# Where the squares for the first norm are taken: from GpSimd to ScalarE and VectorE in a one-core decoder layer

## The chip, the core and the metric

The kernel runs on one core of a Trainium2 chip. The metric is the device time of one execution in microseconds (us). The engines are named as in the profile: PE is TensorE (matmuls), PEld its weight loads, DVE is VectorE, ACT is ScalarE, POOL is GpSimd and SP is the engine that issues the loads. On-chip memory is SBUF, and matmuls add up in PSUM.

## The reference

One decoder layer over 256 tokens of width 2048 and a final norm, in float32. What matters here is how it begins:

```
def rms_norm(x, g):
    xf = x.astype(jnp.float32)
    y = xf * lax.rsqrt(jnp.mean(xf * xf, axis=-1, keepdims=True) + EPS)
    return (y * g.astype(jnp.float32)).astype(x.dtype)
...
        h = rms_norm(x, norm_mix[l])
        z = h @ w_in[l]
        z_a, z_b, z_cq, z_ckv_c, z_ckv_s, z_ckv_w, z_cg = jnp.split(z, split_at, axis=-1)
```

Three token mixers follow on the parts of `z`, then an output product, cross attention, a squared-ReLU MLP and the last norm. The norm's factor is one number for each token, so it can be multiplied in after the product with `w_in`, and that is what the kernel does.

## The kernel before

**Products.** Every product with a weight matrix takes its operands as two float32r parts, hi and lo = x - hi, and sums hi*hi + hi*lo + lo*hi. A weight block of 128 x 1024 numbers (512 KB) is loaded into a tile `raw`; ACT copies it to `wh` (line 82), DVE subtracts to get `wl` (line 83), and only then can PE use it. There are five `raw` buffers and three of `wh` and of `wl`, used in turn. So a load waits until the DVE is done with the block five before it, and ACT's copy waits until PE is done with the block three before it.

**The start.** `x` lies transposed in `xres`, 16 chunks of 128 features by 256 tokens. For each chunk ACT writes `hx` hi = x * gain (line 87) and DVE writes `hx` lo (line 88). The first product, `cmp`, has two accumulators (`cmp_84` and `cmp_85` in the queues below) and runs over four blocks of four chunks beside the loads of `x` and of its own eight weight blocks; the loads of the first two blocks are cut into pieces of one or two chunks. A block of one accumulator takes PE eight pairs of matmuls: one of 256 columns with `wl` (line 165) and one of 512 columns with `wh` (line 161). The second product is `k` (`acc_k0`).

**The norm.** The sum of squares over the features is kept in `ssq` (128 x 512: two chunks at a time). The first pair of chunks is squared into `ssq`; the seven others are squared into `sq` and added. `mean_eps` adds the two halves of `ssq` on POOL (line 112), multiplies by ones on PE (`pss`, line 114) and adds epsilon on DVE (`mx`); `rstd` takes the power on POOL (`rx`); `along_free` spreads it over partitions (`dg`, `psb`, `rxb`). Nothing before `rxb` needs it except the scaling of `cmp` and `k` after their products. Later norms use the same `add_squares` with the squares on ACT and the adds on POOL (lines 102 and 106).

**What sets the order.** The program is written in an order, but a scheduler at build time places the instructions in each engine's queue by its own estimate of when they can run. On the chip each queue is worked off strictly in order. The queues shown below are what it made.

Of the kernel before, what the change touches and what calls it, by code (L numbers as in the profile page):

```python
# [8 lines left out]
F32 = mybir.dt.float32  # L9
# [6 lines left out]
P = 128  # L16
S = 256
# [13 lines left out]
# column blocks of w_in that come out transposed, two 128-wide features a pair  # L31
CMP, UU, KV, CQ, BK, BQ = 0, 2, 4, 6, 10, 12
# the parts that a product in float32r takes: hi*hi, hi*lo, lo*hi
# [4 lines left out]
def trunk_kernel(ctx: ExitStack, tc: tile.TileContext, a, out):  # L38
    """Every product with a weight matrix takes its float32 operands as two float32r parts, hi and
    lo = x - hi (exact), and sums hi*hi + hi*lo + lo*hi in PSUM.  # L40

    Activations that feed a product lie transposed, [features, part, tokens], both parts side by side.
    A product comes out transposed (weights stationary, in two halves: hi*hi + lo*hi and hi*lo) or
    with tokens on partitions (activations stationary)."""
# [15 lines left out]
    # brings the activation table in before the first data  # L60
# [24 lines left out]
    def split_scaled(hi, lo, src, g):  # L85
        """hi + lo = src * g, with g one number a partition."""
        nc.scalar.activation(hi, src, AF.Copy, scale=g)
        nc.vector.scalar_tensor_tensor(lo, src, g, f32(hi), op0=ALU.mult, op1=ALU.subtract)

    def put_act(tiles, k0, src, gi):  # L90
        """src [P, n, S], features k0 .. k0 + n, times their gains."""
        for i in range(src.shape[1]):
            k = k0 + i
            t = tiles[k // 4]
            split_scaled(t[:, k % 4, 0, :], t[:, k % 4, 1, :], src[:, i, :], gT[:, gi, k:k + 1])

# [1 line left out]
    def add_squares(ssq, src, first, eng=None):  # L98
        """ssq [P, 2, S] += src ** 2."""
        sq = ssq if first else sp.tile([P, 2, S], F32, tag="sq", name="sq")  # L100
        if eng is None:
            nc.scalar.activation(sq, src, AF.Square)  # L102
        else:
            eng.tensor_tensor(sq, src, src, op=ALU.mult)
        if not first:
            nc.gpsimd.tensor_tensor(ssq, ssq, sq, op=ALU.add)  # L106

    def mean_eps(ssq, name):
        """mean over features of the squares, + eps: [P tokens, 2]."""
        s = cp.tile([P, 2], F32, name=name)  # L110
        ps = pmisc.tile([P, 2], F32, tag="sc", name="pss")
        nc.gpsimd.tensor_tensor(ssq[:, 0, :], ssq[:, 0, :], ssq[:, 1, :], op=ALU.add)
        for t in range(2):
            nc.tensor.matmul(ps[:, t:t + 1], ssq[:, 0, t * P:(t + 1) * P], ones[:, 0:1], start=True, stop=True)
        nc.vector.tensor_scalar(s, ps, 1.0 / D, EPS, op0=ALU.mult, op1=ALU.add)
        return s
# [6 lines left out]
    def along_free(r, name):  # L123
        """r [P tokens, 2] as [P, S], the same on every partition."""
        b = cp.tile([P, S], F32, name=name)
        ps = pmisc.tile([P, S], F32, tag="sc", name="psb")
        for t in range(2):
            dg = sp.tile([P, P], F32, tag="dg", name="dg")
            nc.vector.tensor_scalar_mul(dg, ident, r[:, t:t + 1])
            nc.tensor.matmul(ps[:, t * P:(t + 1) * P], ones, dg, start=True, stop=True)  # L130
        nc.scalar.activation(b, ps, AF.Copy)
        return b

# [8 lines left out]
    def gemm_t1(x, wsrc, name):  # L142
        """Like gemm_t for a contraction of 512, with one sum: [P, 2 features, tokens]."""
        acc = pacc.tile([P, 2, 2, S], F32, tag="acc", name=name)
        wh, wl = (w.rearrange("p (k n) -> p k n", k=4) for w in split_w(load_raw(wsrc)))
        for kk in range(4):
            for f in range(2):
                fs = slice(f * P, (f + 1) * P)
                for j, (w, l) in enumerate(((wh, 0), (wh, 1), (wl, 0))):
                    nc.tensor.matmul(acc[:, f, 0, :], w[:, kk, fs], x[:, kk, l, :],  # L150
                                     start=(kk == 0 and j == 0), stop=(kk == 3 and j == 2))
        return acc

    def products_t(acc, x, wh, wl, first, last):
        """acc [P, 2 features, hi*hi + lo*hi | hi*lo, tokens] += four 128-row chunks of the contraction."""
        for kk in range(4):
            for f in range(2):
                fs = slice(f * P, (f + 1) * P)

                def main(start, stop):  # L160
                    nc.tensor.matmul(acc[:, f].rearrange("p a s -> p (a s)"), wh[:, kk, fs],  # L161
                                     x[:, kk].rearrange("p a s -> p (a s)"), start=start, stop=stop)

                def low():
                    nc.tensor.matmul(acc[:, f, 0, :], wl[:, kk, fs], x[:, kk, 0, :], start=False, stop=False)  # L165

                if first and kk == 0:
                    main(True, False)
                    low()
                else:  # L170
                    low()
                    main(False, last and kk == 3)

    def gemm_t(lhs, wsrc, name, order=None, between=None):
        """Two 128-wide features, transposed: [P, 2 features, hi*hi + lo*hi | hi*lo, tokens]."""
# [9 lines left out]
    def join(acc, name, dst=None):  # L185
        """The two halves of gemm_t, added."""
# [6 lines left out]
    def gemm(lhs, wsrc, kb, n, name, between=None, hold=0):  # L193
        """Tokens on partitions: [P, 2, n]; blocks of kb 128-row chunks of the contraction. The last
        hold blocks stay, and the first tokens go through all of them before the others."""
# [67 lines left out]
    def consts(them):  # L263
        """Not ahead of the weights asked for so far."""
# [6 lines left out]
    ident = C["ident"]  # L271
    ssq = sp.tile([P, 2, S], F32, tag="ssq", name="ssq")
    for n in range(8):
        add_squares(ssq, xres[:, 2 * n:2 * n + 2, :], n == 0, nc.gpsimd)
# [6 lines left out]
    # nothing is scaled before the norm is there  # L281
    cw = slot("hC", "cw", F32).rearrange("p k a s -> p (k a s)")
    kraw = cw[:, :4 * S].rearrange("p (g s) -> p g s", g=4)
    for m, acc in enumerate(cmps):
        join(acc, "cmp", kraw[:, 2 * m:2 * m + 2, :])
    vs = slot("hC", "vs", F32).rearrange("p k a s -> p (k a s)")
    vcat = vs[:, :1024].rearrange("p (b t n) -> p b t n", b=2, t=2)
    zb = vs[:, 1024:].rearrange("p (t n) -> p t n", t=2)
    kcat = slot("hB", "kcat").rearrange("p (g a) b s -> p g a b s", g=2)
    acc_k0 = gemm_t(hx, a["w_t"][KV], "k0")  # L290
# [15 lines left out]
    # lo, hi and none: one product with hi and one with lo sum what is needed in two halves  # L306
# [6 lines left out]
    def compress():  # L313
        for m, which in enumerate(("k", "v")):
# [7 lines left out]
            # rows 0..29: hi*hi + hi*lo, rows 30..59: lo*hi  # L322
# [26 lines left out]
            else:  # L349
                # v_c of a group at the partitions 32 h of each of its heads  # L350
# [24 lines left out]
    # no compressed block lies before the first rows  # L375
# [8 lines left out]
    def softmax_pair(sc0, sc1, m0, m1, name):  # L384
        """Masked scores of two heads (or branches), both token tiles: exp(s - max) and its sums."""
# [15 lines left out]
    def scale_and_transpose(v0, v1, r, name):  # L401
        """p * r, transposed: [keys, 2, 384], the first 256 columns of keys 0..127, then 128 of the rest."""
# [20 lines left out]
    mix = [None] * 4  # L423
    for g in range(2):
# [5 lines left out]
        # compressed branch, four heads at once  # L430
# [135 lines left out]
    # w_out: the spatial gating's features last; the memory's loads among the products  # L566
# [76 lines left out]
    for q in range(4):  # L643
# [16 lines left out]
        for n in range(4):  # L660
# [3 lines left out]
            for t in range(2):  # L664
# [7 lines left out]
                if q == 3 and n == 2:  # L672
                    # what the last quarter adds comes to this
# [43 lines left out]
def _blocks(w, kb, n):  # L717
    """[K, N] -> [N / n, K / (128 kb), 128, kb * n]: what one partition reads is contiguous."""
    k = w.shape[0]
    return (w.reshape(k // (P * kb), kb, P, -1, n).transpose(3, 0, 2, 1, 4).reshape(-1, k // (P * kb), P, kb * n))  # L720


def _arrays(np, i):
# [15 lines left out]
    # cmp, u, selected k, window k, NSA q, dilated k, dilated q  # L739
# [43 lines left out]
```

## Time and profile before

| | |
|---|---|
| time of three runs | 1216.53 us median (1216.46 to 1218.69) |
| span of the profiled execution, first to last instruction | 1216.0 us |
| PE, DVE, ACT, POOL busy | 1187.0, 750.9, 588.3, 61.3 us |
| matmuls | 6450 |
| HBM read | 221.06 MB |

The profile gives the span of one execution; the three runs give whole times, whose median is 0.5 us longer than that span. Busy shares are averages over the whole program; the start, which is what the change touches, is a stretch of some 45 us of the 1216. Where a view prints "x2", two instructions stand in one row and the time is that of both.

### The profile page before, as it was taken

The page shows a single profiled execution, that of the slowest core. Times are in us where ns is not written, and L with a number is a line of the kernel's source. Part 1 is how long each engine was busy: PE and PEld are TensorE (multiplying, and loading weights), DVE is VectorE, ACT ScalarE, POOL GpSimd, SP SyncE. Part 2 cuts the span into 40 slices and gives each one's busy share as a digit, 9 for nine tenths or more (in the row PEclk, how much of TensorE's full clock was granted, in tenths as well). Part 3 has the DMA queues.
Part 4 walks back from the last instruction along what each step waited for, and adds up shares of the span by engine and source line. Part 5 has one row for each costly group of instructions (what it writes and reads, how often), then busy time and mean ns, then how long its engine had stood idle before and what let it go on. Part 6 is the DMA issues. An engine that isn't in the chain of part 4 may idle for free.

```text
span 1216.0 us, 16456 instructions
## 1 busy us (share of the span) xinstructions
PE 1187.0 (98%) x6450; PEld 1021.3 (84%) x6450; DVE 750.9 (62%) x904; ACT 588.3 (48%) x800; POOL 61.3 (5%) x54
## 2 busy tenths in 40 slices
PE   5999999999999999999999999999999999999996
PEld 4899888888878888988888888888888888888885
DVE  8775788467687565865554556554565555566554
ACT  5464555365565455644433444433444433444443
POOL 7000000000033100200000000000000000000000
PEclk9999999999999999999999999999999999999999
DMA  6676533555657555555666655666556566655663
GB/s 228 196 252 209 157 122 122 182 158 172 190 191 224 176 172 174 181 177 192 189 195 191 191 186 182 192 201 193 187 178 192 191 196 195 186 185 185 195 189 104
DMA packets 65385, 224.24 MB, mean 184 GB/s; under 512 B 7963, under 2 KB 9499, under 8 KB 65179
## 3 DMA queue, kind: packets, MB, share of 16 engines
q1 hardware_dynamic: 65307, 223.19, 57.8%
q8 instruction: 50, 0.82, 0.3%
q14 instruction: 28, 0.23, 0.1%
HBM read 221.06 MB, written 2.10 MB: 184 GB/s over the span
## 4 chain that ended last, share of the span: by engine, by line
PE 91%; DVE 4%; issue 2%; ACT 1%; DMA 1%; SPq 0%; ACTq 0%; POOLq 0%; POOL 0%; DVEq 0%
PE dn L207 27%; PE up L161 20%; PE up L165 10%; PE wo L161 3%; PE cq L161 2%; DVE wl L83 2%; PE xo L150 2%; PE bv L207 2%; PE v L207 2%; PE mv L207 2%; PE wo L165 2%; PE cq L165 1%; PE xq L161 1%; PE mk L161 1%; PE u L161 1%
## 5 line engine op out<-in xcount | busy, mean ns | idle before, releaser
L83 DVE TENSOR_TENSOR wl<-raw,wh 128x1024 fp32r<-128x1024 f32 (+3 forms) x414 | 505.2, 1224 | 350.5 <-ACT wh L82 348.8
L82 ACT ACTIVATE wh<-raw 128x1024 fp32r<-128x1024 f32 (+3 forms) x414 | 428.8, 1038 | 459.9 <-PE dn L207 185.5
L161 PE MATMUL up<-h,wh 128*128 128x512 f32 x1024 | 359.3, 398 | 0.0
L207 PE MATMUL dn<-wh,hid 128*128 128x512 f32 x992 | 306.2, 389 | 0.0
L165 PE MATMUL up<-h,wl 128*128 128x256 f32 x1024 | 282.4, 281 | 0.0
L161 PEld LDWEIGHTS up<-h,wh 128*128 128x128 f32 x1024 | 190.6, 188 | 44.1
L207 PEld LDWEIGHTS dn<-wh,hid 128*128 128x128 f32 x992 | 186.2, 188 | 38.4
L165 PEld LDWEIGHTS up<-h,wl 128*128 128x128 f32 x1024 | 193.3, 189 | 2.7
L207 PE MATMUL dn<-wl,hid 128*128 128x512 f32 x496 | 193.1, 389 | 0.6 <-DVE sf L675 0.6
L207 PEld LDWEIGHTS dn<-wl,hid 128*128 128x128 f32 x496 | 93.1, 188 | 20.5 <-DVE wl L83 1.0
L161 PE MATMUL wo<-mix,wh 128*128 128x512 f32 x256 | 89.5, 395 | 0.4 <-ACT wh L82 0.4
L165 PE MATMUL wo<-mix,wl 128*128 128x256 f32 x256 | 70.7, 282 | 3.3 <-DVE wl L83 3.3
L161 PEld LDWEIGHTS wo<-mix,wh 128*128 128x128 f32 x256 | 47.5, 188 | 10.9 <-ACT wh L82 0.7
L165 PEld LDWEIGHTS wo<-mix,wl 128*128 128x128 f32 x256 | 48.3, 189 | 5.2 <-DVE wl L83 4.5
L188 ACT ACTIVATE half<-up 128x512 f32<-128x512 f32 x32 | 19.1, 597 | 56.7 <-PE up L161 56.7
L161 PE MATMUL cq<-hx,wh 128*128 128x512 f32 x128 | 45.5, 397 | 0.0
L190 DVE TENSOR_TENSOR half<-up,half 128x512 f32<-128x512 f32 x32 | 22.1, 692 | 35.5 <-ACT half L188 35.5
L106 POOL TENSOR_TENSOR ssq<-ssq,sq 128x512 f32<-128x512 f32 x21 | 30.6, 1456 | 174.6 <-ACT sq L102 174.2
L680 POOL TENSOR_TENSOR rf<-sf,mhalf 128x1 f32<-128x1 f32 x2 | 1.1, 560 | 706.8 <-DVE sf L678 706.8
L165 PE MATMUL cq<-hx,wl 128*128 128x256 f32 x128 | 35.3, 281 | 0.0
L161 PE MATMUL cmp<-hx,wh 128*128 128x512 f32 x64 | 27.6, 463 | 4.6 <-ACT wh L82 4.6
L666 DVE SCALAR_TENSOR_TENSOR xt<-dn,m,xt 128x512 f32<-128x512 f32 x32 | 22.6, 747 | 14.3 <-PE dn L207 14.3
(282 smaller groups left out, 1409.9 us busy)
## 6 DMA issues: line engine op xcount, KB each, us to landing
raw<-in_w_up SPq DMA_DIRECT2D x128, 512.0 KB, 4.3
raw<-in_w_down SPq DMA_DIRECT2D x128, 512.0 KB, 4.3
raw<-in_w_t SPq DMA_DIRECT2D x52, 512.0 KB, 3.6
raw<-in_w_out SPq DMA_DIRECT2D x32, 512.0 KB, 4.3
raw<-in_w_bv SPq DMA_DIRECT2D x8, 512.0 KB, 3.7
raw<-in_w_v SPq DMA_DIRECT2D x8, 512.0 KB, 3.5
raw<-in_w_mk SPq DMA_DIRECT2D x8, 512.0 KB, 4.2
raw<-in_w_q SPq DMA_DIRECT2D x8, 512.0 KB, 3.8
```

The lines of the kernel that those rows point to most:

```text
L82: nc.scalar.activation(hi, src, AF.Copy)
L83: nc.vector.tensor_tensor(lo, src, f32(hi), op=ALU.subtract)
L106: nc.gpsimd.tensor_tensor(ssq, ssq, sq, op=ALU.add)
L150: nc.tensor.matmul(acc[:, f, 0, :], w[:, kk, fs], x[:, kk, l, :], start=(kk == 0 and j == 0), stop=(kk == 3 and j == 2))
L161: nc.tensor.matmul(acc[:, f].rearrange("p a s -> p (a s)"), wh[:, kk, fs], x[:, kk].rearrange("p a s -> p (a s)"), start=start, stop=stop)
L165: nc.tensor.matmul(acc[:, f, 0, :], wl[:, kk, fs], x[:, kk, 0, :], start=False, stop=False)
L188: nc.scalar.activation(lo, acc[:, :, 1, :], AF.Copy)
L190: nc.vector.tensor_tensor(d, acc[:, :, 0, :], lo, op=ALU.add)
L207: nc.tensor.matmul(acc[t][:, :n], lhs[k // 4][:, k % 4, l, ts], w[:, kk, :], start=(k == 0 and j == 0), stop=(k == KD - 1 and j == 2))
L666: nc.vector.scalar_tensor_tensor(xs, acc[t], r3[:, t:t + 1], xs, op0=ALU.mult, op1=ALU.add)
L680: nc.gpsimd.tensor_tensor(rf, s_, mhalf[:, 0:1], op=ALU.pow)
```

## The change

The squares of all eight pairs of chunks are taken by ACT (`Square`), and the seven adds for this norm run on DVE. They are written in a generator that the second product calls between its blocks, with the two joins of `cmp` ahead of them; the steps from `mean_eps` to `nrx` are written after the second product. Later norms keep their adds on POOL.

```
-    def add_squares(ssq, src, first, eng=None):
-        """ssq [P, 2, S] += src ** 2."""
+    def add_squares(ssq, src, first, add=None):
         sq = ssq if first else sp.tile([P, 2, S], F32, tag="sq", name="sq")
-        if eng is None:
-            nc.scalar.activation(sq, src, AF.Square)
-        else:
-            eng.tensor_tensor(sq, src, src, op=ALU.mult)
+        nc.scalar.activation(sq, src, AF.Square)
         if not first:
-            nc.gpsimd.tensor_tensor(ssq, ssq, sq, op=ALU.add)
+            (add or nc.gpsimd).tensor_tensor(ssq, ssq, sq, op=ALU.add)
...
     ssq = sp.tile([P, 2, S], F32, tag="ssq", name="ssq")
-    for n in range(8):
-        add_squares(ssq, xres[:, 2 * n:2 * n + 2, :], n == 0, nc.gpsimd)
+
+    def squares():
+        for m, acc in enumerate(cmps):
+            join(acc, "cmp", kraw[:, 2 * m:2 * m + 2, :])
+        for b in range(4):
+            for n in (2 * b, 2 * b + 1):
+                add_squares(ssq, xres[:, 2 * n:2 * n + 2, :], n == 0, add=nc.vector)
+            yield
+
+    acc_k0 = gemm_t(hx, a["w_t"][KV], "k0", between=squares())
     rx = rstd(mean_eps(ssq, "mx"), "rx")
     rxb = along_free(rx, "rxb")
...
-    for m, acc in enumerate(cmps):
-        join(acc, "cmp", kraw[:, 2 * m:2 * m + 2, :])
...
-    acc_k0 = gemm_t(hx, a["w_t"][KV], "k0")
```

Where the scheduler puts this is not where it is written. The first place is DVE's queue during the first product, from block 1 (`hx_81` is the second of the four `hx` tiles) to the weights of block 2 (128x1024). Before:

```order
L88 SCALAR_TENSOR_TENSOR hx_81<-xres,gT,hx_81 128x256 x2
L83 TENSOR_TENSOR wl<-raw,wh 128x512 x2
L88 SCALAR_TENSOR_TENSOR hx_81<-xres,gT,hx_81 128x256 x2
L83 TENSOR_TENSOR wl<-raw,wh 128x512 x2
L88 SCALAR_TENSOR_TENSOR hx_82<-xres,gT,hx_82 128x256 x4
L83 TENSOR_TENSOR wl<-raw,wh 128x1024 x2
```

After the change (the adds have line 103 there):

```order
L88 SCALAR_TENSOR_TENSOR hx_81<-xres,gT,hx_81 128x256 x2
L103 TENSOR_TENSOR ssq<-ssq,sq 128x512
L83 TENSOR_TENSOR wl<-raw,wh 128x512
L88 SCALAR_TENSOR_TENSOR hx_81<-xres,gT,hx_81 128x256
L83 TENSOR_TENSOR wl<-raw,wh 128x512
L88 SCALAR_TENSOR_TENSOR hx_81<-xres,gT,hx_81 128x256
L103 TENSOR_TENSOR ssq<-ssq,sq 128x512
L83 TENSOR_TENSOR wl<-raw,wh 128x512 x2
L88 SCALAR_TENSOR_TENSOR hx_82<-xres,gT,hx_82 128x256 x4
L103 TENSOR_TENSOR ssq<-ssq,sq 128x512 x2
L83 TENSOR_TENSOR wl<-raw,wh 128x1024 x2
```

So four adds stand ahead of the weights of block 2, inside the first product; one more stands ahead of these rows and two behind them. ACT's queue changes in the same way: its eight squares (line 101 after the change) stand behind the `hx` pieces of their own chunks, all in the first product, and no further table load appears.

The second place is PE's queue at the end of the first product. Before, the product with ones stands behind the whole of it:

```order
L161 MATMUL cmp_85<-hx_83,wh 128x512
L165 MATMUL cmp_85<-hx_83,wl 128x256
L161 MATMUL cmp_85<-hx_83,wh 128x512
L114 MATMUL pss<-ones,ssq 128x1 x2
L161 MATMUL k_383<-hx_80,wh 128x512
```

After the change it stands ahead of the last eight pairs:

```order
L158 MATMUL cmp_84<-hx_83,wh 128x512
L162 MATMUL cmp_84<-hx_83,wl 128x256
L158 MATMUL cmp_84<-hx_83,wh 128x512
L111 MATMUL pss<-ones,ssq 128x1 x2
L162 MATMUL cmp_85<-hx_83,wl 128x256
```

It moved forward past eight pairs of matmuls; the matmuls of `psb`, which stood in the second product, moved forward by twelve matmuls. POOL's queue loses its first fifteen tensor instructions. SP's queue, with every load, is the same in both, and so is all that comes behind the second product but for one copy on ACT and one subtraction on DVE that each move by a place.

## Rows read from the trace of the kernel before

**Rows 1.** The page: span, busy time of the engines, POOL's busy tenths by slice.

```profile
span 1216.0 us, 16456 instructions
...
PE 1187.0 (98%) x6450; PEld 1021.3 (84%) x6450; DVE 750.9 (62%) x904; ACT 588.3 (48%) x800; POOL 61.3 (5%) x54
...
POOL 7000000000033100200000000000000000000000
```

**Rows 2.** What PE waited for, whole span: us in total, times, longest.

```profile
PE cmp L165 <- DVE wl L83: 9.7, 4, 3.9
PE cmp L161 <- ACT wh L82: 4.6, 1, 4.6
PE wo L165 <- DVE wl L83: 3.3, 3, 1.7
```

**Rows 3.** Busy us by stretch; the last three columns: granted clock, DMA share, GB/s.

```profile
10.44:11.90 1.46, 0.73 (x4) 0.68 (x5) 1.22 (x3) 0.67 (x2) 0.00 (x0) 1.00 0.92 302
...
17.20:28.50 11.30, 6.91 (x28) 5.16 (x26) 11.30 (x9) 5.74 (x10) 11.08 (x9) 0.85 0.62 199
```

**Rows 4.** DVE by form, 6 to 31 us: count, busy us, mean ns, idle before.

```profile
L88 DVE SCALAR_TENSOR_TENSOR hx<-xres,gT,hx 128x256 fp32r<-128x256 f32 x11 | 13.2, 1244 | 1.6 <-ACT hx L87 1.6
L83 DVE TENSOR_TENSOR wl<-raw,wh 128x512 fp32r<-128x512 f32 x6 | 8.0, 1362 | 0.2 <-ACT wh L82 0.2
```

**Rows 5.** DVE by form, 31 to 62 us.

```profile
L88 DVE SCALAR_TENSOR_TENSOR hx<-xres,gT,hx 128x256 fp32r<-128x256 f32 x4 | 1.7, 472 | 0.0
...
L302 DVE TENSOR_TENSOR cw<-cw,rxb 128x512 f32<-128x512 f32 x2 | 1.3, 690 | 0.4 <-ACT rxb L131 0.4
```

**Rows 6.** DVE in order of time: start, us, instruction, idle time before it.

```profile
8.17 2.35 DVE L88 SCALAR_TENSOR_TENSOR hx<-xres,gT,hx 128x256 fp32r<-128x256 f32 x2 [0.25 <-ACT hx L87]
10.44 0.68 DVE L83 TENSOR_TENSOR wl<-raw,wh 128x512 fp32r<-128x512 f32 x1
...
12.40 2.27 DVE L88 SCALAR_TENSOR_TENSOR hx<-xres,gT,hx 128x256 fp32r<-128x256 f32 x2 [0.34 <-ACT hx L87]
...
28.64 2.88 DVE L83 TENSOR_TENSOR wl<-raw,wh 128x1024 fp32r<-128x1024 f32 x2
...
33.03 1.21 DVE L83 TENSOR_TENSOR wl<-raw,wh 128x1024 fp32r<-128x1024 f32 x1
```

**Rows 7.** ACT's squares of later norms, line 102: least, median, most ns.

```profile
L102 ACT ACTIVATE sq<-xres x14: 617/618/621, 325.3 to 498.3; 128x512 f32<-128x512 f32 x14
```

**Rows 8.** PE in order of time.

```profile
16.17 0.39 PE L165 MATMUL cmp<-hx,wl 128*128 128x256 f32 x1 [1.95 <-DVE wl L83]
...
21.89 0.39 PE L165 MATMUL cmp<-hx,wl 128*128 128x256 f32 x1 [2.37 <-DVE wl L83]
...
30.43 0.58 PE L165 MATMUL cmp<-hx,wl 128*128 128x256 f32 x1 [3.92 <-DVE wl L83]
...
36.27 0.39 PE L161 MATMUL cmp<-hx,wh 128*128 128x512 f32 x1
...
43.90 0.39 PE L161 MATMUL cmp<-hx,wh 128*128 128x512 f32 x1
44.12 0.50 PE L114 MATMUL pss<-ones,ssq 128*128 128x1 f32 x4
```

**Rows 9.** ACT in order of time.

```profile
11.86 0.91 ACT L87 ACTIVATE hx<-xres,gT 128x256 fp32r<-128x256 f32 x2 [0.53 <-DMA xres<-in_xT]
...
14.03 0.91 ACT L87 ACTIVATE hx<-xres,gT 128x256 fp32r<-128x256 f32 x2
14.85 1.17 ACT L82 ACTIVATE wh<-raw 128x512 fp32r<-128x512 f32 x2
...
18.29 1.05 ACT L82 ACTIVATE wh<-raw 128x1024 fp32r<-128x1024 f32 x1
```

**Rows 10.** POOL in order of time: the addition of the two halves of `ssq`.

```profile
28.51 0.79 POOL L112 TENSOR_TENSOR ssq<-ssq 128x256 f32<-128x256 f32 x1
```

**Rows 11.** SP's queue in order of time: the last two loads of the first product.

```profile
13.39 8.80 SPq L253 DMA_DIRECT2D raw<-in_w_t  x2
```

More of the change, by code (lines that the diff above doesn't have):

```diff
@@ L271, in trunk_kernel @@
     ident = C["ident"]
-    ssq = sp.tile([P, 2, S], F32, tag="ssq", name="ssq")
-    for n in range(8):
-        add_squares(ssq, xres[:, 2 * n:2 * n + 2, :], n == 0, nc.gpsimd)
+    cw = slot("hC", "cw", F32).rearrange("p k a s -> p (k a s)")
+    kraw = cw[:, :4 * S].rearrange("p (g s) -> p g s", g=4)
+    vs = slot("hC", "vs", F32).rearrange("p k a s -> p (k a s)")
+    vcat = vs[:, :1024].rearrange("p (b t n) -> p b t n", b=2, t=2)
+    zb = vs[:, 1024:].rearrange("p (t n) -> p t n", t=2)
+    kcat = slot("hB", "kcat").rearrange("p (g a) b s -> p g a b s", g=2)
+    ssq = sp.tile([P, 2, S], F32, tag="ssq", name="ssq")
+    def squares():
[6 more added lines that the diff above has]
+    acc_k0 = gemm_t(hx, a["w_t"][KV], "k0", between=squares())
     rx = rstd(mean_eps(ssq, "mx"), "rx")
@@ L280, in trunk_kernel @@
     nc.vector.tensor_scalar_mul(nrx, rx, -1.0)
-    cw = slot("hC", "cw", F32).rearrange("p k a s -> p (k a s)")
-    kraw = cw[:, :4 * S].rearrange("p (g s) -> p g s", g=4)
-    for m, acc in enumerate(cmps):
-        join(acc, "cmp", kraw[:, 2 * m:2 * m + 2, :])
[L286 to L289, printed above, removed]
-    acc_k0 = gemm_t(hx, a["w_t"][KV], "k0")
     consts([("cau", [P, S]), ("mcmp", [P, 2, NCMP]), ("mB", [P, 384]), ("bs", [P, NB]), ("triu", [P, P])])
```

## The prediction

> **What bounds the kernel now.** I read four views: the page, the list of PE's waits, tables by stretch and by form, and the engines in order of time through the first 45 us. The page shows PE busy for 98% of the span, and POOL busy almost only at the very start [rows 1]. The list of waits says where PE's few idle microseconds are: 9.7 us behind DVE's `wl` and 4.6 us behind ACT's first `wh` (the very first data), both in the first product; the next entry in all that follows is 3.3 us [rows 2]. So whatever the first product gives up moves the rest forward, and there is no slack behind it to swallow the gain.
>
> Inside the first product PE is not short of columns but of split weights, and those come from DVE, which is busy 11.30 of the 11.30 us from 17.20 to 28.50 [rows 3]. It is slow there: an instruction of line 88 on 128x256 takes 1244 ns on average between 6 and 31 us [rows 4] and 472 ns behind 31 us [rows 5]; the 128x512 form of line 83 averages 1362 ns [rows 4], but 0.68 us at 10.44 [rows 6]. That last row decides what to blame. It lies in a gap of POOL: from 10.44 to 11.90 POOL did nothing, the DMA engines were 92% busy, and DVE ran at its normal pace. From 17.20 to 28.50 the DMA share is lower, 0.62, POOL works 11.08 of 11.30 us, and DVE crawls [rows 3]. DVE is slow when POOL works, whatever the loads do.
>
> **The change part by part.**
>
> *Removed from POOL:* eight squares and seven adds, all its tensor work of the first product. None of it is on the path; what counts is that DVE's instructions go back to their undisturbed durations.
>
> *Added:* eight squares on ACT, 617 ns each where the same form runs later [rows 7], and seven adds of 128x512 on DVE. For these the nearest row is line 302, two in 1.3 us [rows 5]; I take 0.66. Both stand inside the first product, not beside the second as they are written, so they count against the path.
>
> A rule speaks against this half of the change. The row has DVE saturated, 11.30 of 11.30 us [rows 3]. The Trainium skill (Perfetto Trace Analysis, section Optimizing Scalar/DVE Operations) advises to take work off a saturated DVE, even to GpSimd, though it doubts that trading between these two helps because they share a read port. By its advice alone, seven adds more on DVE at the durations now seen make the kernel slower, 1220.8; by the rows with and without POOL they are paid back several times, 1206.0. Both are worked out below.
>
> *The path to block 2.* PE's last wait in the first product ends at 30.43 [rows 8], when the first `wl` of block 2 is there: DVE began it, with its twin, at 28.64 [rows 6]. I follow DVE's new queue from the last point that the loads fix. At 11.86 a piece of `x` lands and ACT makes `hx` hi [rows 9]; DVE's line 88 follows at 12.40 [rows 6]. From there to block 2's first `wl` the new queue holds eight of line 88, four 128x512 of line 83, four adds and the 128x1024 itself. Undisturbed, 8 x 0.45 + 4 x 0.64 + 4 x 0.66 + 1.21 = 10.0 us, so it ends at 22.4, and PE starts at 22.5: **7.9 us earlier**. (1.21 is the row at 33.03; 0.45 lies between 1.7 / 4 and 0.472; 0.64 between half of 1.21 and 0.68 [rows 5, 6].) With the lowest of these it is 22.0, with the highest 22.9.
>
> ACT has to keep up. The next piece of `x` was taken without a wait at 14.03, so it had landed. From there ACT's queue to block 2's first `wh` holds two of line 87, three weights of 128x512, four of line 87, three squares and 1.05 us: 0.9 + 1.75 + 1.8 + 1.85 + 1.05 = 7.4 us [rows 7, 9], so 21.4. DVE's queue reaches that `wl` at 22.4 - 1.2 = 21.2. A tie; I stay at 22.4 and allow 1 us above.
>
> *The clock.* Behind 30.43 PE runs without a wait to 44.12, 13.7 us for 32 pairs. At the full clock a pair takes (43.90 - 36.27) / 22 = 0.347 us [rows 8], so 32 take 11.1. The difference of 2.6 us is a stretch at the 1.2 GHz level after waits of 1.95, 2.37 and 3.92 us; the granted clock is already down to 0.85 on average from 17.20 to 28.50 [rows 3]. Now PE restarts block 0 at 10.5 (8.17 plus two of line 88, an add and a `wl`), has done its last eight pairs at 13.3, waits 1.3 us for block 1 at 14.6, and 2.3 us from 20.2 to 22.5 for block 2. Before, it had waited 9.7 - 3.9 = 5.8 us by 22 and fell; now it will have waited some 4.3, with 0.8 ahead of 10.5. I take full speed: **2.6 us gained**.
>
> *The product with ones* costs PE the same at its new place, but it needs the seventh add and 0.79 us on POOL [rows 10]. Behind 22.4 DVE's queue is 1.21 + 4 x 0.45 + 0.66 + 1.21 + 0.66: `wl` of block 3 is there at 27.3, the add at 27.9, POOL's sum at 28.8. PE wants the weights at 22.5 + 16 x 0.347 = 28.1 and the sum at 30.8. Cost zero, hidden behind blocks 2 and 3, with 0.8 and 2.0 us in hand; if either were later, every matmul behind it would wait as long.
>
> *The loads.* The last two weight blocks of the first product were held up on SP, 8.80 us from 13.39 [rows 11], because a `raw` buffer came free only when DVE had split its contents. Now that is done near 17.4. Even with 4 us to land the block is there at 22, wanted by ACT near 26. SP's order is unchanged.
>
> *Sum.* The first product ends at 22.5 + 11.1 = 33.6 instead of 44.12 [rows 8]: 10.5 us, 7.9 of them from DVE and 2.6 from the clock. Behind it the queues are the same but for three single places, and PE was busy there and stays so. The profiled execution's 1216.0 [rows 1] becomes 1205.5; the median of the three runs lies 0.5 above that span, so **1206.0**.
>
> **The rivals.**
>
> *PE at half clock again.* For it: it fell after a wait of 2.37 us [rows 8], and one of 2.3 is left. Against: the sum of waits is smaller. Price: up to the 2.6 us above, so 1208.6; 1207.3 for half of it.
>
> *All at the lower rows.* `wl` at 22.0 and ACT no brake, or `rxb` early enough to save a wait behind: 0.5 to 2 us more, 1204 to 1205.5. For it: four of line 88 take 1.7 us together [rows 5]. Against: ACT's tie.
>
> *DVE gets seven adds and nothing back* (the other side). If the slow stretch comes from the loads or from DVE itself, line 88 stays at 1244, line 83 at 1362, and the adds cost 1362 too: from 12.40, 8 x 1.24 + 4 x 1.36 + 4 x 1.36 + 2.88 / 2 = 22.2, so 34.6 instead of 30.3, 4.3 us later: 1220.8. It decides from the point where line 88 keeps more than about 0.9 us, since 8 x (0.87 + 1.22) + 1.21 fills the time to 30.3. For it: DVE is full. Against: the gap of POOL at 10.44 with the loads at 0.92 [rows 3].
>
> *Something behind takes it back.* The weights of `k` may be no earlier, as every load waits for a buffer and every `wh` for PE; PE would then stand at 34. For it: the buffers couple all engines. Against: they come free on DVE's times, which move forward by the same 8 to 10 us. Half the gain lost is 1211, all of it 1216.5.
>
> **How the numbers follow.** The forecast, 1205.5 to 1207, has 0.52; half clock (1207 to 1209.5) 0.19; the lower rows (1203 to 1205.5) 0.15; taken back (1209.5 to 1217) 0.10, a third of it within 2.4 us of no change; DVE burdened 0.03; 0.01 lies beyond. The range 1203.0 to 1210.0 holds the first three and a little of the fourth. 0.2% (2.4 us) is about what a measurement of this kernel can tell from no change. Faster by more than that 0.93, within it 0.04, slower 0.03.
>
> **What would show it.** In the changed kernel line 88 averages 0.42 to 0.48 us ahead of 31 us, the 128x512 subtraction 0.6 to 0.7, the added lines about 0.66 on DVE and 0.6 on ACT, and POOL does no tensor work before the sum of the halves. PE's last wait in the first product ends near 22.5, `k` starts near 34, and the granted clock stays at the 2.4 GHz level from 10 us on. I am wrong if line 88 stays above 0.9 us with POOL idle, if PE stands ahead of the moved product with ones or of block 3, if ACT and not DVE is what DVE's `wl` waits for over a us, or if a wait of some us stands behind 34 that was not there.

## The result, and the profile of the changed kernel

The changed kernel takes **1206.24 us** (median of four runs, 1205.78 to 1206.72), beside 1217.23 us for the kernel before in the same comparison: a ratio of 0.9901 by the comparison's own estimate, with a 95% interval of 0.9888 to 0.9915 (the two medians alone give 0.9910). The forecast was 1206.0, and its steps can be looked up in the new trace.

The page of the changed kernel, to set against [rows 1]: span, PE's busy time, POOL's busy tenths in 40 slices of 30 us.

```profile
span 1204.7 us, 16460 instructions
...
PE 1183.8 (98%) x6450; PEld 1018.5 (85%) x6450; DVE 743.3 (62%) x911; ACT 592.2 (49%) x808; POOL 42.9 (4%) x39
...
POOL 0000000000123001100000000000000000000000
```

POOL's first slice went from 7 to 0, and DVE, which took over seven adds, is busy for 743.3 us instead of 750.9. With more instructions it works less: its others have become shorter. DVE by form from 6 to 31 us says which, and answers to [rows 4]:

```profile
L88 DVE SCALAR_TENSOR_TENSOR hx<-xres,gT,hx 128x256 fp32r<-128x256 f32 x14 | 6.1, 480 | 1.6 <-ACT hx L87 1.6
...
L103 DVE TENSOR_TENSOR ssq<-ssq,sq 128x512 f32<-128x512 f32 x7 | 4.8, 686 | 0.2
L83 DVE TENSOR_TENSOR wl<-raw,wh 128x512 fp32r<-128x512 f32 x6 | 4.0, 686 | 0.2 <-ACT wh L82 0.2
```

Line 88 fell from 1244 to 480 ns, the 128x512 subtraction from 1362 to 686. The seven adds cost 4.8 us. What that does for PE is in the list of its waits ([rows 2] before):

```profile
PE cmp L158 <- ACT wh L82: 4.3, 1, 4.3
PE wo L162 <- DVE wl L83: 3.1, 3, 1.6
PE cmp L162 <- DVE wl L83: 2.3, 3, 1.6
```

9.7 us behind `wl` in the first product have become 2.3. In PE's order of time (against [rows 8]) these are three waits, and the last ends at 22.00 instead of 30.43:

```profile
10.46 0.39 PE L162 MATMUL cmp<-hx,wl 128*128 128x256 f32 x1 [0.33 <-DVE wl L83]
...
13.93 0.38 PE L162 MATMUL cmp<-hx,wl 128*128 128x256 f32 x1 [0.38 <-DVE wl L83]
...
22.00 0.38 PE L162 MATMUL cmp<-hx,wl 128*128 128x256 f32 x1 [1.63 <-DVE wl L83]
...
30.59 0.50 PE L111 MATMUL pss<-ones,ssq 128*128 128x1 f32 x4
...
33.85 0.40 PE L158 MATMUL k<-hx,wh 128*128 128x512 f32 x1
```

`k`, the second product, starts at 33.85 us. In the trace of before, PE in order of time:

```profile
44.49 0.47 PE L161 MATMUL k<-hx,wh 128*128 128x512 f32 x1
```

So 10.6 of the 11.3 us by which the span is shorter come from the first product, and 0.7 from behind it. The granted clock stands in the last but two column of the busy times by stretch ([rows 3] before); here the stretches 10:20, 20:30 and 30:34:

```profile
10.00:20.00 10.00, 9.22 (x49) 7.29 (x48) 8.83 (x17) 8.33 (x18) 0.00 (x0) 1.00 1.01 391
20.00:30.00 10.00, 8.37 (x49) 7.02 (x48) 8.99 (x13) 7.12 (x11) 1.66 (x1) 1.00 0.88 268
30.00:34.00 4.00, 4.00 (x26) 3.53 (x25) 2.88 (x8) 1.55 (x2) 0.71 (x1) 1.00 0.94 218
```

1.00 in all three is the 2.4 GHz level, where the trace of before shows 0.85 on average from 17.20 to 28.50 and half speed again behind its last long wait, which ended at 30.43. Busy times by stretch, before:

```profile
32.00:36.00 4.00, 4.00 (x15) 3.42 (x14) 2.24 (x4) 0.04 (x1) 0.00 (x0) 0.51 0.79 266
```

### The profile page after: what moved, and what is told of

It reads as the page before. It is cut to its first block, busy times and chain, and to the rows that moved or that the text cites. A ratio compares the mean times of both kernels' runs of the same rounds, so it can differ in the third digit from the quotient of the medians.

```text
span 1204.7 us, 16460 instructions
## 1 busy us (share of the span) xinstructions
PE 1183.8 (98%) x6450; PEld 1018.5 (85%) x6450; DVE 743.3 (62%) x911; ACT 592.2 (49%) x808; POOL 42.9 (4%) x39
## 4 chain that ended last, share of the span: by engine, by line
PE 92%; DVE 3%; DMA 2%; issue 1%; ACT 1%; SPq 0%; ACTq 0%; POOLq 0%; POOL 0%; DVEq 0%
PE dn L204 27%; PE up L158 20%; PE up L162 10%; PE wo L158 3%; PE cq L158 2%; PE xo L147 2%; PE bv L204 2%; PE v L204 2%; PE mv L204 2%; PE wo L162 2%; DVE wl L83 1%; PE cq L162 1%; PE xq L158 1%; PE u L158 1%; PE bk L158 1%
## 5 line engine op out<-in xcount | busy, mean ns | idle before, releaser
L158 PE MATMUL cmp<-hx,wh 128*128 128x512 f32 x64 | 25.1, 431 | 4.3 <-ACT wh L82 4.3
L82 ACT ACTIVATE hid<-half 128x512 fp32r<-128x512 f32 x32 | 20.2, 632 | 17.1 <-DVE half L651 17.1
L158 PEld LDWEIGHTS cq<-hx,wh 128*128 128x128 f32 x128 | 23.9, 188 | 5.1
```

The lines of the kernel that those rows point to most:

```text
L82: nc.scalar.activation(hi, src, AF.Copy)
```

## The experiments

A theory had to be told apart from its rivals. Mine: POOL's work beside DVE holds up DVE's instructions, and PE waits for DVE. The rivals: it is the work itself that counts (moved to where there is room), or its place in the program (beside the first or the second product). A finer question is whether POOL's being busy is enough, or whether it has to read SBUF. Each comparison carries its own runs of the kernel before, whose medians lay between 1216.8 and 1218.0.

**a_adds_pool: only half of the change.** The squares are on ACT, the adds stay on POOL.

```diff
-                add_squares(ssq, xres[:, 2 * n:2 * n + 2, :], n == 0, add=nc.vector)
+                add_squares(ssq, xres[:, 2 * n:2 * n + 2, :], n == 0)
```

> Squares on ACT as changed, but the seven adds stay on POOL: half of POOL's tensor work of the first product is back. Theory (POOL's work slows DVE): seven adds of about 1.4 us are 10 us of POOL work instead of 20, each holding DVE up by some 0.8 us (1244 - 472 ns); DVE itself loses the adds. From 12.4 to block 2's first wl 8 x 0.45 + 4 x 0.64 + 1.21 = 7.4 us and four or five hold-ups of 0.8, so 23.0 to 23.6 instead of 22.0: 1207 to 1209 us, line 88 at 0.6 to 0.9 us ahead of 31 us. Rival (the slow stretch came from the loads or from DVE itself): DVE has the queue of the kernel before, so 1216 to 1217.

Measured: 1208.78 us (1207.61 to 1209.32), ratio 0.9932 [0.9918, 0.9946]. With half of POOL's reading left, line 88 stands about halfway between 480 and 1244 ns (DVE by form, 6 to 31 us):

```profile
L88 DVE SCALAR_TENSOR_TENSOR hx<-xres,gT,hx 128x256 fp32r<-128x256 f32 x15 | 11.1, 789 | 2.4 <-ACT hx L87 2.4
```

PE waits 4.2 us for `cmp`'s `wl` instead of 2.3, and the clock is near its lower level twice, at 0.53. Busy times by stretch:

```profile
11.80:15.30 3.50, 3.50 (x13) 2.98 (x12) 2.18 (x3) 3.28 (x8) 1.28 (x1) 0.53 1.05 420
25.50:28.90 3.40, 3.40 (x12) 2.88 (x12) 3.40 (x5) 0.45 (x1) 2.60 (x2) 0.53 0.81 258
```

So the seven adds cost 4.8 us when they are on DVE, and having them there is still worth 2.5 us of the kernel's time (by the medians of two comparisons), which is the opposite of what a count of DVE's work says.

**c_junk_reads: POOL's reading put back, with no use.** The changed kernel, and beside it 15 multiplications of 128x512 on POOL whose result nobody reads. The other engines' work is unchanged.

```diff
+    junk = cp.tile([P, 2, S], F32, name="junk")
+    nc.gpsimd.memset(junk, 0.0)
+    for i in range(15):
+        nc.gpsimd.tensor_tensor(junk, junk, xres[:, 0:2, :], op=ALU.mult)
```

> The changed kernel with fifteen multiplications of 128x512 on POOL whose result nobody uses, from about 6 us on; the queues of DVE, ACT and PE are those of the changed kernel. Theory: line 88 is back at 1.2 us and the adds on DVE take about 1.36, block 2's first wl comes at 34 to 35, the clock falls again: 1219 to 1223 us, slower than the kernel before. Rival (the gain came from the new order of the queues and from the moved product with ones): 1206 to 1207, the product with ones at most 1 or 2 us late behind POOL's queue.

Measured: 1217.82 us (1216.08 to 1219.36), ratio 1.0005 [0.9996, 1.0015]: the whole gain is gone. DVE by form from 6 to 28.5 us, while the multiplications ran:

```profile
L88 DVE SCALAR_TENSOR_TENSOR hx<-xres,gT,hx 128x256 fp32r<-128x256 f32 x7 | 10.0, 1450 | 0.9 <-ACT hx L87 0.9
L83 DVE TENSOR_TENSOR wl<-raw,wh 128x512 fp32r<-128x512 f32 x4 | 6.9, 1753 | 0.0
L103 DVE TENSOR_TENSOR ssq<-ssq,sq 128x512 f32<-128x512 f32 x2 | 3.5, 1760 | 0.0
```

POOL's side of the same time, 6 to 31 us:

```profile
L279 POOL TENSOR_TENSOR junk<-junk,xres 128x512 f32<-128x512 f32 x15 | 21.6, 1441 | 5.1 <-DMA xres<-in_xT 4.0
```

Each of DVE's instructions took about its own time plus one of POOL's: line 88's 0.48 us and 1.04 us, which one such multiplication takes when it starts before DVE (it is in d_junk_writes below), make 1.52 for the 1.45 seen, and line 83's 0.69 and 1.04 make 1.73 for 1.75. That is what two engines that take turns would give.

The time came out 1 us under the range, although PE started block 2 at 34.81, as expected. The multiplications were over at 28.5 us, and the granted clock fell once only (0.50 from 26 to 32 us) and was at 1.00 from 33 us on, so PE ran from that start at full speed; in the kernel before it ran there at 0.51. So the new order of the queues is not what gains, and POOL's work need not be of any use to take the gain back. Whether it is POOL's reading or its being busy, this run does not tell; the next one does.

**d_junk_writes: POOL as busy, but only writing.** One operation that reads, and then 40 memsets of the same 128x512.

```diff
+    nc.gpsimd.tensor_tensor(junk, xres[:, 0:2, :], xres[:, 0:2, :], op=ALU.mult)
+    for i in range(40):
+        nc.gpsimd.memset(junk, 0.0)
```

> The same with forty memsets of 128x512 on POOL, which write SBUF and read nothing, about 0.5 us each, 16 to 20 us in all over the first product. If any work of POOL holds DVE up, line 88 is above 1 us again and the kernel takes 1214 to 1222 us. If only reading does (as the Trainium skill, SBUF - State Buffer, section on its two separate sides, has it for DVE instructions with two SBUF inputs), line 88 stays at 0.48 and the time at 1206 us, within 1 us.

Measured: 1205.3 us (1204.23 to 1208.17), ratio 0.9908 [0.9893, 0.9923], the time of the changed kernel. DVE by form and POOL by form, both from 6 to 31 us:

```profile
L88 DVE SCALAR_TENSOR_TENSOR hx<-xres,gT,hx 128x256 fp32r<-128x256 f32 x15 | 7.0, 508 | 1.4 <-ACT hx L87 1.4
...
L83 DVE TENSOR_TENSOR wl<-raw,wh 128x512 fp32r<-128x512 f32 x6 | 4.0, 689 | 0.0
```

```profile
L279 POOL MEMSET junk<- 128x512 f32 x37 | 19.5, 526 | 2.1
...
L277 POOL TENSOR_TENSOR junk<-xres 128x512 f32<-128x512 f32 x1 | 1.0, 1040 | 3.8 <-DMA xres<-in_xT 3.8
```

19.5 us of POOL's work cost DVE nothing (the mean of 508 ns holds one of 0.90 us at 5.57, beside the one operation that reads). "POOL is busy" is not the cause; that it reads SBUF is. (POOL's reading work in all these runs has two inputs; no run tried one with a single input.)

**e_behind: the squares where the text has them.** In the changed kernel they stand in the code beside the second product, but the scheduler put them inside the first. Here they are queued on ACT behind the first product's last weight copy (`last` in the cut below), and the adds run on DVE from 25.1 to 35.1 us.

```diff
+                with tc.issue_after(last):
+                    add_squares(ssq, xres[:, 2 * n:2 * n + 2, :], n == 0, add=nc.vector)
```

> The squares as they are written in the change: queued on ACT behind the last weight copy of the first product, so squares and adds stand beside the second product. Theory: DVE's queue to block 2's first wl loses four adds and ACT's three squares; wh of block 2 at about 19.5, wl at 20.8, PE starts 1.1 to 1.6 us earlier than 22.0; if DVE has room in the second product the kernel takes 1204.6 to 1205.6 us. Rival (the place that the scheduler chose is part of the gain): the norm's factor comes late, DVE is full from 34 to 50 us, PE waits there: 1207 to 1211 us.

Measured: 1210.54 us (1210.25 to 1211.31), ratio 0.9949 [0.9936, 0.9961]. My expectation failed and the rival held. The first product did get faster (`k` at 31.16), but the norm came late. ACT's copy of `rxb`, and PE in the product that follows on the second one (its tiles are named `k` too), both in order of time:

```profile
46.82 0.37 ACT L130 ACTIVATE rxb<-psb 128x256 f32<-128x256 f32 x1
```

```profile
52.92 0.58 PE L164 MATMUL k<-hx,wl 128*128 128x256 f32 x1 [3.87 <-DVE wl L85]
```

In the changed kernel, ACT in order of time:

```profile
37.80 0.37 ACT L128 ACTIVATE rxb<-psb 128x256 f32<-128x256 f32 x1
```

There PE waits for nothing in this product. In e_behind what is scaled by `rxb` stands in one piece ahead of the next `wl`, 3.6 us of DVE's work from 48.09 on. PE waits 3.87 us, and the granted clock is 0.50 from 51 to 57. DVE's piece is not the whole of that wait. ACT's copy and DVE's subtraction for the block that PE waits for, both in order of time:

```profile
49.08 1.06 ACT L84 ACTIVATE wh<-raw 128x1024 fp32r<-128x1024 f32 x1 [1.89 <-PE k L160]
```

```profile
51.66 1.21 DVE L85 TENSOR_TENSOR wl<-raw,wh 128x1024 fp32r<-128x1024 f32 x1
```

The copy ended at 50.14, so DVE's piece cost 1.5 us. The other 2.3 passed because the copy began only when PE had finished the block before. Of the three `wh` buffers the other two, by the order in which they are used, held weights of the product `ph`, which needs the norm (its operand `blk` is made from what `rxb` has scaled) and ran from 58.06 on (in the changed kernel from 48.20).

**b_all_dve: squares and adds both on DVE.** POOL and ACT have none of it.

```diff
-        nc.scalar.activation(sq, src, AF.Square)
+        if add is None:
+            nc.scalar.activation(sq, src, AF.Square)
+        else:
+            add.tensor_tensor(sq, src, src, op=ALU.mult)
```

> Squares and adds both on VectorE, GpSimd idle, ScalarE without squares. Theory (only GpSimd's reading held VectorE up): line 88 stays at 0.45 to 0.55 us and a 128x512 subtraction at 0.69; VectorE carries eight squares of about 0.69 us more, four of them ahead of block 2's first wl, so TensorE starts block 2 some 2 to 3 us later than the 22.0 of the changed kernel, near 24.5, and then half a us to a us goes at block 3: 1208.5 to 1211 us. Rival 1 (it only counts that GpSimd is left, whoever takes the work): 1206, the same as the changed kernel. Rival 2 (VectorE full with all of the work is no better than the kernel before): 1215 to 1218.

Measured: 1213.7 us (1212.4 to 1214.27), ratio 0.9966 [0.9954, 0.9978]: slower than my range, and the price lay elsewhere than I had put it. Line 88 is at 479 ns. DVE is busy for 19.86 of the 20 us from 10 to 30, yet PE starts block 2 at 22.19, as in the changed kernel, and `k` at 33.61. PE in order of time:

```profile
22.19 0.38 PE L165 MATMUL cmp<-hx,wl 128*128 128x256 f32 x1 [1.30 <-DVE wl L83]
...
33.61 0.39 PE L161 MATMUL k<-hx,wh 128*128 128x512 f32 x1
...
36.42 0.50 PE L114 MATMUL pss<-ones,ssq 128*128 128x1 f32 x4
...
45.34 0.60 PE L130 MATMUL psb<-dg,ones 128*128 128x128 f32 x4
...
54.87 0.58 PE L165 MATMUL k<-hx,wl 128*128 128x256 f32 x1 [3.33 <-DVE wl L83]
```

The last add ends at 31.9 instead of 27.0, so PE's products with ones stand behind the first block of `k`, and `rxb` comes at 46.98, 9.2 us later than in the changed kernel. About 4 of these 9 us are added by places in PE's queue: POOL's sum was there at 32.70 and `pss` ran at 36.42, `dg` was there at 39.33 and `psb` ran at 45.34 (in the changed kernel 28.74 and 30.59, 32.59 and 36.64). It is the same lateness as in e_behind, again with a wait of over 3 us, and a granted clock of 0.82 and 0.75 in the 8 us behind 52. Taking work off POOL pays even when all of it goes to DVE, but the squares on ACT are worth another 7.5 us. The first product is as fast without that, so the loss lies behind it, where the norm is late.

**f_pool_behind: all of it on POOL, but beside the second product.** A tiny operation ahead of them in POOL's queue reads the first product's sums; `add_squares` is that of b_all_dve.

```diff
+        go = nc.gpsimd.tensor_tensor(gate_, kraw[:, 0, 0:2], kraw[:, 0, 0:2], op=ALU.mult)
...
+                with tc.issue_after(go.ins):
+                    add_squares(ssq, xres[:, 2 * n:2 * n + 2, :], n == 0, add=nc.gpsimd)
```

> All fifteen squares and adds stay on GpSimd, but a tiny operation that reads the first product's sums stands ahead of them in GpSimd's queue, so that they run beside the second product, where the changed kernel's text has them. Theory (VectorE is held up wherever GpSimd reads beside it, and the norm is late): the first product is as fast as with no squares at all (block 2 starts near 21, k near 33), but from 33 to about 55 us line 83 and line 88's neighbours on VectorE take about twice their time, the 128x1024 subtraction 2.2 us or more instead of 1.2, rxb comes 15 us or more later than 37.8, and TensorE waits 5 us or more in the second product and what follows: 1212 to 1222 us. Rival (the contention matters only in the first product, where VectorE is short): 1204.5 to 1206.

Measured: 1223.04 us (1221.79 to 1224.62), ratio 1.0046 [1.0029, 1.0063]: slower than before, 1 us over my range. The first product was fast (`k` at 31.82). Then POOL reads from 30.65 to 56.5, and DVE in order of time shows whom it holds up:

```profile
32.84 0.68 DVE L190 TENSOR_TENSOR cw<-cmp,half 128x512 f32<-128x512 f32 x1
...
35.90 2.23 DVE L83 TENSOR_TENSOR wl<-raw,wh 128x1024 fp32r<-128x1024 f32 x1 [1.00 <-ACT wh L82]
...
43.76 0.69 DVE L190 TENSOR_TENSOR half<-k,half 128x512 f32<-128x512 f32 x1 [0.40 <-ACT half L188]
```

The subtraction of line 83 takes 2.23 us instead of 1.22, but line 190, which adds a PSUM tile and one SBUF tile, keeps its 0.69. And the norm is 25 us late (`rxb` at 62.36), for which PE stands still, in the list of its waits:

```profile
PE ph L339 <- DVE blk L83: 6.5, 1, 6.5
PE k L165 <- DVE wl L83: 4.6, 2, 3.4
...
PE psb L130 <- DVE dg L129: 2.3, 1, 2.3
```

So POOL's reading holds DVE up beside either product, and together with the late norm it costs more than the first product gives; this run does not part the two.

**h_own_block: each block's squares behind that block's weights.** A middle way between the changed kernel and e_behind: two squares fewer ahead of block 2's `wl` (`ends[b]` is the last weight copy of block b).

```diff
+                with tc.issue_after(ends[b]):
+                    add_squares(ssq, xres[:, 2 * n:2 * n + 2, :], n == 0, add=nc.vector)
```

> The changed kernel with the squares of each block queued on ScalarE behind the last weight copy of their own block, so that two squares and a VectorE add or two fewer stand ahead of block 2's first wl, and the norm is hardly later. Theory (VectorE's queue sets block 2's start): block 2's first wl and TensorE's start come 0.7 to 1.5 us earlier than 22.0, and as rxb is later by under 2 us nothing behind waits for it: 1204.5 to 1205.5. Rival (what is gained there is lost behind, as with the squares queued behind the first product): 1206 to 1208.

Measured: 1206.25 us (1205.87 to 1207.2), ratio 0.9909 [0.9894, 0.9924]: no gain, the rival held. Both halves are in PE's order of time:

```profile
20.76 0.38 PE L162 MATMUL cmp<-hx,wl 128*128 128x256 f32 x1 [1.06 <-DVE wl L83]
...
49.50 0.38 PE L162 MATMUL k<-hx,wl 128*128 128x256 f32 x1 [1.53 <-DVE wl L83]
```

Block 2 starts 1.24 us earlier, as expected, and 1.53 us are lost at 49.50. `rxb` is 1.4 us later (39.23), and DVE is busy for 12.00 of the 12 us from 40 to 52, as it is in the changed kernel too. So PE arrives earlier at weights that are not earlier: DVE begins that subtraction at 48.24, and the one in its place in the changed kernel at 47.92. Behind the first product DVE has no slack either.

**g_no_pool_adds, i_later_only, after_again, g_again: the same cause elsewhere.** In both kernels the adds of three later norms are on POOL, 21 in all; two of these norms lie beside the `w_out` product (325 to 370 us and further on), the third at 468 to 490 us, where PE hardly waits (0.2 us at `xo`, in g too). g moves all 21 to DVE in the changed kernel (the diff below, and g_again is the same kernel); i does it in the kernel before and leaves the first norm as it was there; after_again is the changed kernel.

```diff
-            (add or nc.gpsimd).tensor_tensor(ssq, ssq, sq, op=ALU.add)
+            (add or nc.vector).tensor_tensor(ssq, ssq, sq, op=ALU.add)
```

> The changed kernel with the adds of the later norms on VectorE too, where they are on GpSimd in both kernels (325 to 368 us and further on). Theory: the few waits of TensorE on VectorE's wl at line 162 beside these adds (3.1 us in all, with line 83's 128x1024 at 1366 ns there and line 88 at 609 to 702) come of the same contention and shrink to under 1 us, the 128x1024 subtraction goes to 1.2 us, and the time to 1203 to 1205.5. Rival (TensorE is the bound there and VectorE gets the work back that it sheds): within 0.5 us of the changed kernel, 1205.5 to 1206.7; slower than that if the 16 or more adds make VectorE late.

> The kernel before, with only the adds of the two later norms moved from GpSimd to VectorE (the first norm stays on GpSimd as it was). Theory (GpSimd's reading costs wherever TensorE waits for VectorE's wl, and the two places are independent): the first product is slow as before (k starts near 44.5), the waits of TensorE at line 165 in the w_out product (3.3 us before) go, with 0.4 at line 161, so 1212.5 to 1214 us, and the gains of the two places add up to that of the kernel that has both. Rival (the 3.6 us by which the kernel with both beat the changed one came from elsewhere, such as earlier loads): 1216 to 1218.

> The changed kernel once more, beside the next one on the same chip: 1205.5 to 1207 us.

> The changed kernel with the later norms' adds on VectorE too, beside the changed kernel on the same chip: if the waits at the w_out product are what it saves, 3 to 4 us less than the changed kernel in this same call, 1202 to 1203.5; if the difference was one of chips, under 1 us less.

Measured: g 1202.62 us (1201.22 to 1204.13), ratio 0.9882 [0.9861, 0.9902]. In a second comparison, on one chip: before 1217.95, i 1214.16 (1212.63 to 1214.73; ratio 0.9966 [0.9953, 0.9979]), the changed kernel 1205.37 (1204.75 to 1206.72; 0.9900 [0.9883, 0.9917]), g 1201.74 (1201.54 to 1203.14; 0.9869 [0.9855, 0.9883]). The two places add up: 3.8 us for i and 12.6 for the change make 16.4, and g has 16.2. Four of these times lie a little outside what I had expected, by 0.1 to 0.4 us: both of g and that of the changed kernel below it, that of i above it. DVE by form from 300 to 375 us, first of the changed kernel and then of g:

```profile
L83 DVE TENSOR_TENSOR wl<-raw,wh 128x1024 fp32r<-128x1024 f32 x26 | 35.0, 1366 | 9.6 <-ACT wh L82 9.6
...
L88 DVE SCALAR_TENSOR_TENSOR h<-xres,gT,h 128x256 fp32r<-128x256 f32 x14 | 9.3, 702 | 0.0
```

```profile
L83 DVE TENSOR_TENSOR wl<-raw,wh 128x1024 fp32r<-128x1024 f32 x28 | 34.2, 1233 | 8.7 <-ACT wh L82 8.7
...
L88 DVE SCALAR_TENSOR_TENSOR h<-xres,gT,h 128x256 fp32r<-128x256 f32 x14 | 6.1, 481 | 0.0
```

PE's busy time in that stretch, of the changed kernel and of g (the second number is the length, the third PE's):

```profile
300.00:375.00 75.00, 71.14 (x405) 61.20 (x404) 60.41 (x70) 46.84 (x71) 21.04 (x14) 1.00 0.62 204
```

```profile
300.00:375.00 75.00, 75.00 (x431) 65.42 (x431) 61.62 (x87) 48.17 (x73) 1.44 (x2) 1.00 0.64 214
```

The 3.9 us of idle PE, listed as waits for `wo`, are gone (0.4 of them are left in g_again), and i's list has none behind `wl` there either. g is the fastest version here.

## Why the prediction was right, point by point

**DVE was slow because of POOL.** Right, and shown by c, which takes the gain back with work on POOL alone, and by d, in which as much work that does not read takes nothing back. The gap of POOL in [rows 6] was the right row to read. The rival in which DVE gets the adds and nothing back would have needed line 88 above 0.9 us; it is at 0.48. A refinement that the prediction lacked: POOL has to read (d), and DVE's instruction has to take two inputs from SBUF (line 190 in f). The Trainium skill states both conditions (SBUF — State Buffer, section SBUF: two separate sides): the ports are a lock that a VectorE operation with two SBUF inputs contends for, against a GpSimd operation that reads SBUF; the rows of c, d and f agree.

**Durations.** A little low: 480 ns for 450, 686 for 640 and 660, 1.22 us for 1.21.

**Block 2's `wl` at 22.4, PE at 22.5.** Measured 22.00. The queue from line 88 on took 10.5 us instead of 10.0, of which DVE idled 0.7, but it began at 11.39 instead of 12.40, since ACT got that piece of `x` at 10.85 instead of 11.86. So the 8.4 us gained here, for 7.9, come in part of a piece that happened to land a microsecond earlier. In the runs with this same queue that row of line 88 begins anywhere from 11.01 (d_junk_writes) to 12.62 (g_again), and after_again, the same program, started block 2 at 21.16: executions differ by a microsecond here.

**ACT as a tie.** ACT's two copies for block 2 took 2.00 us from 19.41, so the first ended near 20.4, a microsecond ahead of the 21.4 worked out; ACT was no brake.

**The clock.** Right in kind, a little large: the three stretches from 10 to 34 us are all at 1.00, but from block 2's start to `k` PE took 11.85 us (22.00 to 33.85) instead of 14.06 (30.43 to 44.49), which is 2.2 us and not 2.6. A pair of matmuls took 0.353 us there (23 of them from 22.22 to 30.35), not the 0.347 of the prediction; why is open. The waits ahead of block 2's end were smaller than foreseen, 0.33, 0.38 and 1.63 us for 0.8, 1.3 and 2.3. What the rival of half clock would have looked like is in a, where waits of 1.92 and 2.31 us were each followed by a stretch at 0.53.

**The product with ones.** Hidden, as claimed, but one term was mis-sized: POOL's sum of the halves took 1.66 us, not 0.79, in POOL's order of time:

```profile
27.08 1.66 POOL L109 TENSOR_TENSOR ssq<-ssq 128x256 f32<-128x256 f32 x1 [25.75 <-DVE ssq L103]
```

A 128x1024 subtraction that DVE had begun at 26.92 ran beside it (in [rows 10] POOL's sum had begun first); in f, with DVE idle, it took 0.73. It still ended at 28.7, ahead of PE's 30.59.

**The loads.** The last two were 4.34 us on SP instead of 8.80, and nothing waited for them.

**The sum.** The first product gave 10.6 us for 10.5, as 8.4 and 2.2 for 7.9 and 2.6, so that it fits this well is partly luck. Two more errors hid each other: the span fell by 11.3, because 0.7 came from behind the first product, and the time around the span was taken as 0.5 us from a median, where the profiled execution shows 2.0 (1206.72 beside 1204.7). What exactly gave the 0.7 was not tried; it is within what executions of one program differ by here (spans of 1204.7 and 1202.8 for the changed kernel).

**What the prediction did not see** is what the place is worth. It took the scheduler's placing as a cost (the adds "count against the path"). b and e show the other side: with the squares later, or on DVE, `rxb` comes 9 us later, and the time is 4.3 and 7.5 us longer although `k` starts as early or earlier. "Something behind takes it back" did not happen in the changed kernel. Where it does, in b and e, it begins with the norm's time, which the rival did not name, and reaches PE through DVE's queue and, for 2.3 of e's 3.87 us, through the `wh` buffers, which it did name.

## What to carry to other kernels

When VectorE is full and its instructions take two to three times the duration that the same form has elsewhere, look for what GpSimd reads at that time; moving the reading work onto the busy engine itself can pay, since 4.8 us of adds bought back 11 x 0.76 + 6 x 0.68 = 12.5 us on the instructions of [rows 4]. Then look for the same pair in the other stages: the list of TensorE's waits named the second place (`wo`) before any experiment. And before moving a chain of small work out of a tight stretch, ask who consumes its end: in e_behind `k` started 2.7 us earlier and the span was still 4.6 us longer, with a norm that came 9 us later.

## What the runs showed that was not expected

GpSimd's memsets beside VectorE cost neither engine anything that shows: 37 of 128x512 at 526 ns each (0.52 us for one that ran at 0.73 us, ahead of VectorE's work, in c_junk_reads), with line 83 at 689 ns beside them. An addition on VectorE with one input in PSUM keeps its 0.68 to 0.69 us beside a reading GpSimd, while a subtraction with both in SBUF takes 2.23 us for 1.22. Both sides of the contention pay: GpSimd's own 128x256 addition took 0.73 us with VectorE idle and 1.66 beside a subtraction on VectorE.
